# Input projection of a hybrid decoder layer in five column groups instead of six, one of them loaded in two parts

## The chip, the cores and the metric

The kernel runs on one core of a Trainium2 chip. One program does both layers. The metric is the device time of one execution in microseconds (us). One core has five engines that run their own instruction streams in order: PE (TensorE, matrix products; PEld are its weight loads), DVE (VectorE), ACT (ScalarE), POOL (GpSimd) and SP (SyncE), which here only issues DMA transfers. They wait for each other by semaphores.

## The reference

Two layers on x of 256 tokens by 1024, all in float32. The change touches only the input projection, the product of `h` with `w_in` (1024 by 3476 columns per layer), whose columns are split among the three head groups:

```
for l in range(DEPTH):
    h = rmsnorm(x, norm_mix[l])
    proj = jnp.einsum('bsd,de->bse', h, w_in[l]).astype(jnp.float32)
    (m_q, m_k, m_v, m_o, m_i, m_f, b_q, b_k, b_v,
     n_q, n_kc, n_vc, n_ks, n_vs, n_kw, n_vw, n_g) = jnp.split(proj, SPLIT_POINTS, axis=-1)
    ...
    gif = jnp.concatenate([m_i, m_f], axis=-1) + b_if[l]
    y_m = mlstm(..., gif[..., :M_HEADS], gif[..., M_HEADS:], m_norm[l])
    y_b = moba(b_q, b_k, b_v, ...)
    y_n = nsa(n_q, n_kc, n_vc, n_ks, n_vs, n_kw, n_vw, n_g, ...)
    mix = jnp.concatenate([y_m, y_b, y_n], axis=-1).astype(x.dtype)
    x = x + jnp.einsum('bse,ed->bsd', mix, w_out[l])
    h = rmsnorm(x, norm_ffn[l])
    u = jnp.square(jax.nn.relu(jnp.einsum('bsd,df->bsf', h, w_ff1[l])))
    x = x + jnp.einsum('bsf,fd->bsd', u, w_ff2[l])
```

## The kernel before

**How a weight reaches PE.** Weights come in pieces of at most 128 partitions by 1024 elements. For each piece SP issues a DMA into a buffer `raw` (5 buffers), ACT casts it to a rounded copy `hi` (6 buffers), DVE subtracts to get the rest `lo` (6 buffers), and PE makes three passes over it: hi with the high part of the activations H, lo with it, hi with the low part. A `raw` buffer is free once its `lo` is made; `hi` and `lo` are free once PE has used them. The compression weights (`whole`, 2 buffers, two DMAs each into its left and its right half) go to PE uncast.

**How the input projection is staged.** `ORDER` lists, per layer, groups of columns (o1 to o6, each in four pieces of 256 rows of `w_in`), transposed groups (q0 to q3, 256 columns in two pieces) and compression steps (c0 to c3). A group o1 to o6 makes 48 matmuls into two PSUM banks, one for each half of the tokens: 2 halves x 8 blocks of rows x 3 passes, as wide as the group. The pool `acc` has two banks, so the next group takes a bank as soon as it has been read and freed. o1 holds the NSA queries and two compression inputs (384 columns), o6 the mLSTM output gates (512), o2 the other NSA keys, values and gates (268), o3 the mLSTM gate inputs and the MoBA queries (8 + 256 = 264).

**Who reads the banks.** `cmp_inputs` reads o1 into `KV` and `R` (ACT). `nsa_heads(l, i)` reads o2's bank of half i: two ACT copies (`R`, `VS`) and one DVE operation (`GT`), then normalizes (`th`, `hss`, `hr`, `N`) and has PE transpose `N` and `KV`. `gates(l)` reads o3: one DVE operation (`GI`, which needs the small load `BIF`) and one ACT copy into a fresh `R` buffer (2 buffers in the pool). `gates` begins only when the second part of `small_loads` has been read: C, BIF, `sel` (through `th` into `SEL`), CW and MN.

**What sets the order.** Every step is a generator that yields operations; class `Flow` keeps a clock for each engine from estimated costs and picks the next operation greedily, by rank where several could start. It also writes the order of SP's transfers. All instructions go through one helper, so the profile shows line L137 for all of them and L136 for all DMA issues; tiles tell them apart.

Of the kernel before, what the change touches and what calls it, by code (L numbers as in the profile page):

```python
# [10 lines left out]
AF = mybir.ActivationFunctionType  # L11
ALU = mybir.AluOpType
# [9 lines left out]
C_MQ, C_MK, C_MV, C_MO, C_G, C_BQ, C_BK, C_NQ, C_KS = 0, 512, 1024, 1536, 2048, 2056, 2312, 2824, 3208  # L22
# [4 lines left out]
K_ID, K_TRI, K_NM, K_NMT, K_NMC, K_COS, K_SIN, K_VAL, K_CS, K_END = 0, 128, 256, 384, 512, 544, 576, 608, 612, 868  # L27


ORDER = ("o1", "o6", "o2", "o3", "c0", "c1", "q0", "c2", "c3", "o4", "q1", "q2", "q3", "o5")  # L30

RAW_BUFS, PART_BUFS, AHEAD = 5, 6, 1.3

# [111 lines left out]
class Flow:  # L145
# [25 lines left out]
    def free(self, *tiles):  # L171
        for t in tiles:
            name = t.tensor.name
            self.places[self.owner.pop(name)].append(self.used.get(name, ("", 0.0))[1])
# [108 lines left out]
def body(ctx, tc, x, w_in, b_if, conv_qk, m_norm, moba_g, nsa_qg, nsa_kg, cmp_pe, cmp_w1, cmp_w2,  # L283
# [26 lines left out]
    def keep(tag, *shape, dt=F32, parts=128):  # L310

        if tag not in kept:
            kept[tag] = cp.tile([parts, *shape], dt, tag=tag, name=tag)
        return kept[tag]
# [60 lines left out]
    def rows(w, k0, kk, c0, n):  # L375
        return [(w[k0 * 128:(k0 + kk) * 128, c0:c0 + n].rearrange("(k p) n -> p k n", p=128), None)], kk, n

    GROUPS = {"o1": (C_NQ, 384), "o2": (C_KS, 268), "o3": (C_G, 264), "o4": (C_BK, 512), "o5": (C_MV, 512),
              "o6": (C_MO, 512)}
    WO_ORDER = [6, 7, 4, 5, 0, 1, 2, 3]  # L380
    NCH = DFF // 256

# [9 lines left out]
    pieces, due = [], []  # L392
    t = 0.0
    for l in range(DEPTH):
        for name in ORDER:
            if name[0] == "c":
                s = int(name[1])
                pieces.append(([(cmp_w1[l, a, s * 512:(s + 1) * 512, :].rearrange("(k p) n -> p k n", p=128), a)
                                for a in range(2)], 8, 128))
                due.append(t)  # L400
                t += 0.45
            elif name[0] == "q":
                pieces += [rows(w_in[l], 4 * s, 4, int(name[1]) * 256, 256) for s in range(2)]
                due += [t, t + 12 * 288 / 2400]
                t += 48 * 288 / 2400
            else:
                n = GROUPS[name][1]
                pieces += [rows(w_in[l], 2 * s, 2, *GROUPS[name]) for s in range(4)]
                due += [t + 6 * s * (n + 32) / 2400 for s in range(4)]
                t += 48 * (n + 32) / 2400  # L410
        pieces += [rows(w_out[l], k, 1, 0, D) for k in WO_ORDER]
        due += [t + 6 * k * 544 / 2400 for k in range(4)] + [t + (48 + 3 * k) * 544 / 2400 for k in range(4)]
        t += 96 * 544 / 2400
        for kind, c, a in FF_ORDER:
            if kind == "up":
                pieces.append(rows(w_ff1[l], 4 * a, 4, c * 256, 256))
                due.append(t)
                t += (8 * 544 + 8 * 288) / 2400
            else:
                if a == 0:  # L420
                    pieces += [rows(w_ff2[l], 2 * c + f, 1, 0, D) for f in range(2)]
                    due += [t, t + 3 * 544 / 2400]
                t += 12 * 544 / 2400

    whole = {j for j, p in enumerate(pieces) if len(p[0]) == 2}
    raws, parts = {}, {}
    coming = [0, 0]
    taken = [0]
# [1 line left out]
    def loads(unsplit):  # L430

        for j, (srcs, kk, n) in enumerate(pieces):
            if (j in whole) != unsplit:
                continue
            if j < 4:
                yield f"before {j}"
            elif unsplit:
                yield f"raw {j - 1}"
            raw = yield new("whole" if j in whole else "raw", 1024)
            raws[j] = raw  # L440
            for src, a in srcs:
                dst = raw[:, :kk * n] if a is None else raw[:, a * 512:(a + 1) * 512]
                yield sy.dma_start(dst.rearrange("p (k n) -> p k n", n=n), src)
            done.add(f"raw {j}")

    def chunks(j):
# [74 lines left out]
    class Layer:  # L521
        def __init__(self):
            self.o, self.held, self.W, self.Y = {}, {}, {}, {}
            self.rs = [keep(f"rs{i}", 1) for i in range(2)]
            self.r2 = [keep(f"r2{i}", 1) for i in range(2)]
            for name, shape, dt in (("H", (8, 2, S), F32R), ("Mh", (8, S), F32R),
                                    ("Ml", (8, S), F32R), ("QK", (10, S), F32), ("RB", (S,), F32),
                                    ("VS", (2, 2, 64), F32), ("VB", (2, 256), F32), ("VM", (2, 4, 130), F32),
                                    ("VC", (4, 64), F32), ("KCT", (2, 16), F32), ("em", (2, 4), F32),
                                    ("cg", (2, 64), F32), ("mr", (384,), F32R)):  # L530
                setattr(self, name, keep(name, *shape, dt=dt))
            self.GT = [keep(f"GT{i}", 12) for i in range(2)]

            self.Hh, self.Hl = (self.H[:, :, a, :] for a in range(2))
            self.Fh, self.Fl = self.Hh, self.Hl

    Ls = [Layer() for _ in range(DEPTH)]

# [360 lines left out]
    def cmp_inputs(l):  # L899
        L = Ls[l]  # L900
        L.R = []
        KV = []
        for i in range(2):
            yield f"o1{l}{i}"
            yield f"rs{l}{i}"
            o = L.o["o1"][i]
            KV.append((yield new("KV", 2, 2, 64)))
            yield act(KV[i], o[:, 256:384].rearrange("p (a d) -> p a d", a=2)[:, :, None, :].to_broadcast([128, 2, 2, 64]),
                      AF.Copy, scale=L.rs[i])
            L.R.append((yield new("R", 8, 64)))  # L910
            yield act(L.R[i][:, 0:4].rearrange("p a d -> p (a d)"), o[:, 0:256], AF.Copy, scale=L.rs[i])
            free(o)
            done.add(f"R{l}{i}")
        yield f"s0{l}"

        Xt = yield new("MQ", 2048)
        yield gp.memset(Xt[:, :1024], 0.0)
        X = Xt[:, :1024].rearrange("p (i a c) -> p i a c", i=16, a=2)
        for a in range(2):
            kt = yield wk(S)  # L920
            for i in range(2):
                yield tr(kt[:, tokens(i)], KV[i][:, a].rearrange("p b d -> p (b d)"), ident)
            for j in range(2):
                src = kt[64 * j:64 * j + 64, :]
                src = bass.AP(tensor=src.tensor, offset=src.offset + j, ap=[src.ap[0], [2, 16], [16, NCMP]])
                yield tt(X[64 * j:64 * j + 64, :, a, :NCMP], src,
                         PEs[64 * j:64 * j + 64, l, a, :][:, :, None].to_broadcast([64, 16, NCMP]), op=ALU.add)
            free(kt)
        free(*KV)
        L.Xt, L.X = Xt, X  # L930
        done.add(f"X{l}")


    def nsa_heads(l, i):
        L = Ls[l]
        yield f"R{l}{i}"
        yield f"o2{l}{i}"
        yield f"s0{l}"
        o, R, GT = L.o["o2"][i], L.R[i], L.GT[i]
        kv = o[:, 0:256].rearrange("p (a b d) -> p a b d", a=2, b=2)  # L940
        yield act(R[:, 4:6], kv[:, :, 0, :], AF.Copy, scale=L.rs[i])
        yield act(L.VS[:, i], kv[:, :, 1, :], AF.Copy, scale=L.rs[i])

        yield ts(GT, o[:, 256:268], L.rs[i], 0.5, op0=ALU.mult, op1=ALU.mult)
        free(o)
        N = yield new("N", 10, 64)
        yield from normed(N, R[:, 0:6], 6, i, ((0, 4, 2, 1), (4, 2, 4, 2)))
        free(R)
        yield copy(N[:, 6:10, 16:64], N[:, 0:4, 16:64])
        yield from rope(N[:, 4:6], N[:, 4:6], 2, i)  # L950

        K = yield new("KV", 2, 2, 64)
        yield copy(K, N[:, 4:6, None, :].to_broadcast([128, 2, 2, 64]))
        yield from rope(N[:, 6:10], N[:, 0:4], 4, i)
        yield from blocks(L, [N[:, 0:2], N[:, 2:4], K[:, 0], K[:, 1], N[:, 6:8], N[:, 8:10]], 4, i)
        free(N, K)
        yield act(GT, GT, AF.Tanh)
        yield ts(GT, GT, 0.5, 0.5, op0=ALU.mult, op1=ALU.add)
        done.add(f"qkn{l}{i}")
# [43 lines left out]
    def gates(l):  # L1003
# [3 lines left out]
        yield f"s1{l}"  # L1007
        L.R2 = []
        for i in range(2):
            yield f"o3{l}{i}"  # L1010
            yield f"rs{l}{i}"
            o = L.o["o3"][i]
            yield stt(GI[:, i], o[:, 0:8], L.rs[i], BIFs[:, l], op0=ALU.mult, op1=ALU.add)
            L.R2.append((yield new("R", 8, 64)))
            yield act(L.R2[i][:, 0:4].rearrange("p a d -> p (a d)"), o[:, 8:264], AF.Copy, scale=L.rs[i])
            free(o)
            done.add(f"bq{l}{i}")
        fg = GI[:, :, 4:8]
        lf, fa, cg, em, BC = keep("lf", 2, 4), keep("fa", 2, 4), L.cg, L.em, keep("BC", 2, 4)
# [364 lines left out]
```

## Time and profile before

| | |
|---|---|
| median of 3 runs | 640.31 us (639.86 to 641.04) |
| the profiled execution's own time | 639.9 us |
| its span | 638.1 us |
| PE busy | 631.1 us, 99% of the span |
| DVE busy | 443.7 us, 70% |
| ACT busy | 367.0 us, 58% |
| granted TensorE clock, whole span | 1.00 |

The span is the part of the execution that the trace covers; 1.8 us of the profiled execution lie around it. Busy shares are of the span.

### The profile page before, as it was taken

The numbers are of one execution on the slowest core, as the hardware profiler recorded it, in microseconds if no ns is written. First come the engines' busy times: TensorE is split into PE (matmuls) and PEld (weight loads), VectorE is DVE, ScalarE is ACT, GpSimd is POOL, SyncE is SP. The second block draws the span as 40 slices with busy tenths as digits, with TensorE's granted clock in tenths as the row PEclk, the third lists the DMA queues.
The fourth block names the chain that finished last, engine by engine and source line by source line (L and its number), as shares of the span: only waits on it lengthen the run. The fifth ranks groups of instructions, "written<-read, shape, count | busy, mean of one in ns | idle before, by whom it ended". The sixth has DMA issues, their size and how long they took to land.

```text
span 638.1 us, 10222 instructions
## 1 busy us (share of the span) xinstructions
PE 631.1 (99%) x3799; PEld 543.9 (85%) x3799; DVE 443.7 (70%) x823; ACT 367.0 (58%) x718; POOL 29.8 (5%) x50
## 2 busy tenths in 40 slices
PE   8999999999999999999999999999999999999997
PEld 8888898888888888888899979988888888888885
DVE  6679898779575665656593979987776565665661
ACT  7679785556463545445474985945645553545440
POOL 1110200100000000000010111001000000000000
PEclk9999999999999999999999999999999999999999
DMA  8886514448556564656446926145466556564611
GB/s 313 235 287 217 164 67 133 131 133 264 193 185 210 165 213 156 225 166 187 142 140 208 318 68 181 52 133 159 155 214 209 187 185 210 167 215 156 223 33 67
DMA packets 79378, 112.78 MB, mean 177 GB/s; under 512 B 4928, under 2 KB 61792, under 8 KB 79328
## 3 DMA queue, kind: packets, MB, share of 16 engines
q1 hardware_dynamic: 79152, 112.05, 55.4%
q8 instruction: 30, 0.49, 0.3%
q14 instruction: 20, 0.16, 0.1%
q10 hardware_dynamic: 176, 0.07, 0.0%
HBM read 111.06 MB, written 1.05 MB: 176 GB/s over the span
## 4 chain that ended last, share of the span: by engine, by line
PE 95%; DMA 2%; DVE 1%; ACT 1%; issue 0%; POOL 0%; ACTq 0%; DVEq 0%; POOLq 0%
PE wk L137 57%; PE acc L137 38%; DMA raw<-in_w_in 1%; DVE lo L137 1%; DMA ident<-in_cst 1%; ACT hi L137 0%; DVE N L137 0%; POOL rs L137 0%; DVE dg L137 0%; DVE x L137 0%; DVE hss L137 0%; DVE t L137 0%; DVE KC L137 0%; ACT th L137 0%; ACTq L136 0%
## 5 line engine op out<-in xcount | busy, mean ns | idle before, releaser
L137 DVE TENSOR_TENSOR lo<-raw,hi 128x1024 fp32r<-128x1024 f32 (+4 forms) x209 | 240.2, 1166 | 124.1 <-ACT hi L137 122.3
L137 ACT CAST hi<-raw 128x1024 fp32r<-128x1024 f32 (+3 forms) x207 | 205.8, 1015 | 133.3 <-PE wk L137 112.1
L137 PE MATMUL wk<-H,hi 128*128 128x512 f32 x512 | 128.0, 391 | 0.0
L137 PEld LDWEIGHTS wk<-H,hi 128*128 128x128 f32 x512 | 93.7, 188 | 17.9
L137 PE MATMUL acc<-hi,H 128*128 128x512 f32 (+3 forms) x368 | 100.0, 352 | 0.0
L137 PE MATMUL acc<-hi,P 128*128 128x512 f32 x240 | 79.2, 391 | 0.0
L137 PE MATMUL wk<-hi,P 128*128 128x512 f32 x240 | 78.8, 389 | 0.0
L137 PEld LDWEIGHTS wk<-H,lo 128*128 128x128 f32 x512 | 69.9, 190 | 5.0
L137 PE MATMUL wk<-H,lo 128*128 128x256 f32 x512 | 71.4, 282 | 0.0
L137 PEld LDWEIGHTS acc<-hi,H 128*128 128x128 f32 x368 | 63.9, 188 | 6.7 <-issue 0.4
L137 PE MATMUL acc<-lo,H 128*128 128x512 f32 (+3 forms) x184 | 65.2, 354 | 0.0
L137 PEld LDWEIGHTS wk<-hi,P 128*128 128x128 f32 x240 | 45.0, 188 | 9.4
L137 PEld LDWEIGHTS acc<-hi,P 128*128 128x128 f32 x240 | 45.2, 188 | 8.9
L137 PE MATMUL acc<-H,hi 128*128 128x256 f32 x256 | 51.3, 292 | 0.0
L137 PE MATMUL acc<-lo,P 128*128 128x512 f32 x120 | 47.0, 392 | 0.0
L137 PE MATMUL wk<-lo,P 128*128 128x512 f32 x120 | 46.7, 389 | 0.0
L137 ACT COPY th<-wk 128x256 f32<-128x256 f32 x64 | 23.8, 373 | 35.7 <-PE wk L137 35.7
L137 PEld LDWEIGHTS acc<-H,hi 128*128 128x128 f32 x256 | 40.4, 191 | 0.9 <-issue 0.5
L137 PEld LDWEIGHTS acc<-lo,H 128*128 128x128 f32 x184 | 34.6, 188 | 3.6 <-issue 0.7
L137 PE MATMUL acc<-H,lo 128*128 128x256 f32 x128 | 37.4, 292 | 0.1
L137 ACT ACTIVATE H<-wk,V 128x128 fp32r<-128x128 f32 x64 | 18.1, 375 | 21.0 <-PE wk L137 21.0
L137 DVE TENSOR_TENSOR cx<-wk,th 128x256 f32<-128x256 f32 x64 | 26.9, 421 | 2.2 <-ACT th L137 2.2
(199 smaller groups left out, 790.7 us busy)
## 6 DMA issues: line engine op xcount, KB each, us to landing
raw<-in_w_ff SPq DMA_DIRECT2D x128, 512.0 KB, 4.4
raw<-in_w_in SPq DMA_DIRECT2D x40, 512.0 KB, 5.0
raw<-in_w_out SPq DMA_DIRECT2D x16, 512.0 KB, 3.7
whole<-in_cmp_w SPq DMA_DIRECT2D x16, 256.0 KB, 4.9
raw<-in_w_in SPq DMA_DIRECT2D x8, 384.0 KB, 4.0
raw<-in_w_in SPq DMA_DIRECT2D x8, 268.0 KB, 3.5
raw<-in_w_in SPq DMA_DIRECT2D x8, 264.0 KB, 3.3
out<-x SPq DMA_DIRECT2D x4, 256.0 KB, 2.0
```

Source lines behind the costliest of these rows:

```text
L137: o = Op(self.name, lambda: f(out, *args, **kw), outs, ins, self.cost(op, outs, ins))
```

## The change

o3 goes away. o1 takes 64 columns of o2 (the key `ks`) and is 448 wide. What is left of o2 (204 columns) and the 264 of o3 become one group o2 of 468 columns. They are not adjacent in `w_in`, so each of its four pieces is loaded by two DMAs: for each of its two row blocks k, columns 0 to 203 of the piece come from the one and columns 204 to 467 from the other. In the buffer the two parts thus alternate: 204, 264, 204, 264.

`nsa_heads` and `gates` both read o2's bank, and `Layer.read` frees it at the second of the two readers. `cmp_inputs` makes one more copy, of 64 columns, into `R`.

```diff
-ORDER = ("o1", "o6", "o2", "o3", "c0", "c1", "q0", "c2", "c3", "o4", "q1", "q2", "q3", "o5")
+ORDER = ("o1", "o6", "o2", "c0", "c1", "q0", "c2", "c3", "o4", "q1", "q2", "q3", "o5")
...
-    GROUPS = {"o1": (C_NQ, 384), "o2": (C_KS, 268), "o3": (C_G, 264), "o4": (C_BK, 512), "o5": (C_MV, 512),
-              "o6": (C_MO, 512)}
+
+    GROUPS = {"o1": (C_NQ, 448), "o2": (C_KS + 64, 468), "o4": (C_BK, 512), "o5": (C_MV, 512), "o6": (C_MO, 512)}
...
-                pieces += [rows(w_in[l], 2 * s, 2, *GROUPS[name]) for s in range(4)]
+                if name == "o2":
+                    pieces += [([(w_in[l, 256 * s:256 * s + 256, c0:c0 + m].rearrange("(k p) n -> p k n", p=128),
+                                      slice(at, at + m)) for c0, m, at in ((C_KS + 64, 204, 0), (C_G, 264, 204))], 2, n)
+                                   for s in range(4)]
+                else:
+                    pieces += [rows(w_in[l], 2 * s, 2, *GROUPS[name]) for s in range(4)]
...
-                dst = raw[:, :kk * n] if a is None else raw[:, a * 512:(a + 1) * 512]
-                yield sy.dma_start(dst.rearrange("p (k n) -> p k n", n=n), src)
+                dst = raw[:, a * 512:(a + 1) * 512] if j in whole else raw[:, :kk * n]
+                dst = dst.rearrange("p (k n) -> p k n", n=n)
+                yield sy.dma_start(dst[:, :, a] if isinstance(a, slice) else dst, src)
...
+            self.left = [2, 2]
...
+        def read(self, i):
+
+            self.left[i] -= 1
+            if not self.left[i]:
+                free(self.o["o2"][i])
...
+            yield act(L.R[i][:, 4], o[:, 384:448], AF.Copy, scale=L.rs[i])
...
-        yield act(R[:, 4:6], kv[:, :, 0, :], AF.Copy, scale=L.rs[i])
-        yield act(L.VS[:, i], kv[:, :, 1, :], AF.Copy, scale=L.rs[i])
-
-        yield ts(GT, o[:, 256:268], L.rs[i], 0.5, op0=ALU.mult, op1=ALU.mult)
-        free(o)
+        yield act(R[:, 5], o[:, 64:128], AF.Copy, scale=L.rs[i])
+        yield act(L.VS[:, i], o[:, 0:256].rearrange("p (a b) -> p a b", a=2)[:, :, 0:64], AF.Copy, scale=L.rs[i])
+
+        yield ts(GT, o[:, 192:204], L.rs[i], 0.5, op0=ALU.mult, op1=ALU.mult)
+        L.read(i)
...
-            yield f"o3{l}{i}"
+            yield f"o2{l}{i}"
             yield f"rs{l}{i}"
-            o = L.o["o3"][i]
-            yield stt(GI[:, i], o[:, 0:8], L.rs[i], BIFs[:, l], op0=ALU.mult, op1=ALU.add)
+            o = L.o["o2"][i]
+            yield stt(GI[:, i], o[:, 204:212], L.rs[i], BIFs[:, l], op0=ALU.mult, op1=ALU.add)
             L.R2.append((yield new("R", 8, 64)))
-            yield act(L.R2[i][:, 0:4].rearrange("p a d -> p (a d)"), o[:, 8:264], AF.Copy, scale=L.rs[i])
-            free(o)
+            yield act(L.R2[i][:, 0:4].rearrange("p a d -> p (a d)"), o[:, 212:468], AF.Copy, scale=L.rs[i])
+            L.read(i)
```

The planner's order moves in three places. The first is SP's list of transfers in layer 0, from o2's first piece on. Names in brackets are the semaphores that an instruction waits for; DMAHW0 to DMAHW7 are raised by landed transfers, the transfers taking them in turn, and the last number is no time. Before, eight transfers load o2 and o3 (the eighth, alike, stands four rows further):

```order
L136 DMA raw_311<-in_w_in 128x2x268 [waits DMAHW6_49,DVE_49]
L136 DMA raw_336<-in_w_in 128x2x268 [waits DMAHW7_49,DVE_49]
L136 DMA raw_355<-in_w_in 128x2x268 [waits DMAHW0_49,DVE_49]
L136 DMA dg_378<-in_cmp_pe 64x128 [waits DMAHW1_49,PE_49]
L136 DMA raw_367<-in_w_in 128x2x268 [waits DMAHW2_49,DVE_49]
L136 DMA raw_387<-in_w_in 128x2x264 [waits DMAHW3_49,DVE_49]
L136 DMA raw_402<-in_w_in 128x2x264 [waits DMAHW6_49,DMAHW4_49,DVE_49]
L136 DMA raw_408<-in_w_in 128x2x264 [waits DMAHW7_49,DMAHW5_49,DVE_49]
```

Of the change, the same place, where each `raw` is filled by two transfers:

```order
L136 DMA raw_306<-in_w_in 128x2x204 [waits DMAHW6_49,DVE_49]
L136 DMA raw_306<-in_w_in 128x2x264 [waits DMAHW7_49,DMAHW6_49]
L136 DMA raw_333<-in_w_in 128x2x204 [waits DMAHW0_49,DVE_49]
L136 DMA raw_333<-in_w_in 128x2x264 [waits DMAHW1_49,DMAHW0_49]
L136 DMA raw_353<-in_w_in 128x2x204 [waits DMAHW2_49,DVE_49]
L136 DMA dg_368<-in_cmp_pe 64x128 [waits DMAHW3_49,PE_49]
L136 DMA raw_353<-in_w_in 128x2x264 [waits DMAHW4_49,DMAHW2_49]
L136 DMA raw_380<-in_w_in 128x2x204 [waits DMAHW5_49,DVE_49]
L136 DMA raw_380<-in_w_in 128x2x264 [waits DMAHW5_49]
```

A transfer's own semaphore is the first one that it waits for in the first column (the one that it reuses): the first 204 raises DMAHW6, the second DMAHW0, the third DMAHW2 and the fourth DMAHW5. Each 264 therefore waits until the 204 of its own buffer has landed; before, no transfer of this stretch waits for one issued just ahead of it. Behind these rows now come the four `whole`, q0's two pieces and o4's first, and only then C, BIF and `sel`, which before stood ahead of o3's last piece. Layer 1 has the same four pairs.

The second place is ACT, layer 0, around the copies out of o2's and o3's banks (rs0 and rs1 are the scales of the two halves of the tokens). Before, `R_635` reads o3's first bank (acc_571) with three of the casts of q0 and o4 ahead of it:

```order
L137 ACTIVATE VS_74<-acc_525,rs1_94 128x128
L137 CAST hi_559<-raw_467 128x1024 [waits DMAHW0_49]
L137 ACTIVATE th_590<-R_384 128x384 [waits Activation_49]
L137 CAST hi_585<-raw_501 128x1024 [waits DMAHW1_49]
L137 COPY N_540<-N_540 128x4x48 [waits DVE_49]
L137 CAST hi_627<-raw_509 128x1024 [waits DMAHW2_49,PE_49]
L137 COPY KV_638<-N_540 128x256 [waits DVE_49]
L137 ACTIVATE R_635<-acc_571,rs0_93 128x256
```

Of the change, `R_613` reads o2's first bank (acc_487); hi_538, hi_554, hi_567 and hi_580 are the casts of o4's four pieces, and q0's two stand ahead of these rows:

```order
L137 CAST SEL_77<-th_448 128x512 [waits DMAHW0_49]
L137 ACTIVATE R_340<-acc_487,rs0_93 128x64 [waits PE_49]
L137 ACTIVATE VS_74<-acc_487,rs0_93 128x128 [waits DVE_49]
L137 ACTIVATE th_542<-R_340 128x384 [waits Activation_49]
L137 CAST hi_538<-raw_426 128x1024 [waits DMAHW5_49,PE_49]
L137 CAST hi_554<-raw_465 128x1024 [waits DMAHW1_49,PE_49]
L137 CAST hi_567<-raw_477 128x1024 [waits DMAHW2_49,PE_49]
L137 CAST hi_580<-raw_499 128x1024 [waits DMAHW3_49,PE_49]
L137 ACTIVATE R_370<-acc_528,rs1_94 128x64
L137 ACTIVATE VS_74<-acc_528,rs1_94 128x128
L137 ACTIVATE R_613<-acc_487,rs0_93 128x256 [waits DVE_49,Activation_49]
```

All four casts of o4 now stand ahead of the copy, and `VS` waits for DVE, which is `GI` and with it BIF. Layer 1 has the same rows but for `SEL`.

The third place is PE, layer 0, at the end of o2 and the start of q0, of the change. acc_615, q0's, is the place that o2's first bank (acc_487) leaves, so that its first matmul waits for `R_613`:

```order
L137 MATMUL acc_528<-hi_463,H_70 128x468
L137 MATMUL wk_579<-whole_393,MQ_433 32x128 [waits DMAHW7_49,Pool_49]
L137 MATMUL wk_579<-whole_393,MQ_433 32x128 [waits DMAHW0_49]
L137 MATMUL wk_579<-whole_393,MQ_433 32x128 x6
L137 MATMUL wk_579<-whole_403,MQ_433 32x128 [waits DMAHW1_49]
L137 MATMUL wk_579<-whole_403,MQ_433 32x128 [waits DMAHW2_49]
L137 MATMUL wk_579<-whole_403,MQ_433 32x128 x6
L137 MATMUL acc_615<-H_70,hi_475 128x256 [waits PE_49,Activation_49]
```

Before, the rows between `whole` and q0 held two transposes of `N` and two of `KV`; these four now come after 24 of q0's 48 matmuls.

## Rows read from the trace of the kernel before

**Rows 1.** Page, part 1: busy time, share of the span, instructions.

```profile
span 638.1 us, 10222 instructions
...
PE 631.1 (99%) x3799; PEld 543.9 (85%) x3799; DVE 443.7 (70%) x823; ACT 367.0 (58%) x718; POOL 29.8 (5%) x50
```

**Rows 2.** Chain that ended last, 0 to 60 us: start, us, what.

```profile
30.16 7.76 DMA raw<-in_w_in
```

**Rows 3.** Timeline of PE, layer 0: start, us, instruction.

```profile
13.02 0.33 PE L137 MATMUL acc<-lo,H 128*128 128x384 f32 x1
...
14.58 0.36 PE L137 MATMUL acc<-lo,H 128*128 128x384 f32 x1
...
26.66 0.62 PE L137 MATMUL acc<-hi,H 128*128 128x512 f32 x2
...
28.02 0.62 PE L137 MATMUL acc<-hi,H 128*128 128x512 f32 x2
...
29.05 0.28 PE L137 MATMUL acc<-lo,H 128*128 128x268 f32 x1
...
40.67 1.08 PE L137 MATMUL wk<-whole,MQ 128*32 128x128 f32 x32
...
42.48 0.51 PE L137 MATMUL acc<-H,hi 128*128 128x256 f32 x2
...
45.44 0.83 PE L137 MATMUL wk<-QK 64*128 64x128 f32 x10
```

**Rows 4.** Timeline of ACT, layer 0: start, us, instruction, idle before.

```profile
27.48 0.62 ACT L137 CAST SEL<-th 128x512 fp32r<-128x512 f32 x1 [0.40 <-DMA th<-in_sel]
...
32.04 0.37 ACT L137 ACTIVATE R<-acc,rs 128x128 f32<-128x128 f32 x1 [1.64 <-PE acc L137]
...
33.65 0.52 ACT L137 ACTIVATE th<-R 128x384 f32<-128x384 f32 x1
...
41.96 0.47 ACT L137 ACTIVATE R<-acc,rs 128x256 f32<-128x256 f32 x1
42.33 1.99 ACT L137 CAST hi<-raw 128x1024 fp32r<-128x1024 f32 x2
```

**Rows 5.** Tile raw, 26.4 to 26.8 us: o3's last piece.

```profile
L136 SPq DMA_DIRECT2D raw<-in_w_in x1: 379/379/379, 26.5 to 26.5; - x1
...
DMA to landing us min/median/max: 3.0/3.0/3.0
```

**Rows 6.** Timeline of SP, layer 0: start, us, transfers issued.

```profile
15.35 3.06 SPq L136 DMA_DIRECT2D raw<-in_w_in  x3
...
26.89 1.03 SPq L136 DMA_DIRECT2D whole<-in_cmp_w  x2
```

**Rows 7.** Tile raw, 15.2 to 15.7 us: o2's first piece.

```profile
L136 SPq DMA_DIRECT2D raw<-in_w_in x1: 379/379/379, 15.4 to 15.4; - x1
...
DMA to landing us min/median/max: 5.0/5.0/5.0
```

**Rows 8.** Groups by form, 5 to 60 us: busy us, mean ns, idle before.

```profile
L137 ACT CAST hi<-raw 128x1024 fp32r<-128x1024 f32 x12 | 12.5, 1061 | 2.4 <-DMA raw<-in_w_in 2.4
...
L137 DVE TENSOR_TENSOR lo<-raw,hi 128x1024 fp32r<-128x1024 f32 x11 | 13.2, 1216 | 0.6 <-ACT hi L137 0.6
```

**Rows 9.** Windows: length, busy PE, PEld, DVE, ACT, POOL, PEclk, DMA, GB/s.

```profile
32.00:40.00 8.00, 8.00 (x68) 8.00 (x68) 3.38 (x9) 4.88 (x10) 1.34 (x1) 1.00 1.03 337
```

**Rows 10.** Layer 1, timelines of SP and PE.

```profile
321.98 18.98 SPq L136 DMA_DIRECT2D raw<-in_w_in  x9
...
343.12 0.28 PE L137 MATMUL acc<-lo,H 128*128 128x268 f32 x1
```

**Rows 11.** What SP waited for, 320 to 341 us: total, times, longest.

```profile
SPq L136 <- DVE lo L137: 23.8, 8, 9.6
```

**Rows 12.** Window at the end, behind the last matmul; columns as in rows 9.

```profile
633.50:638.00 4.50, 0.00 (x0) 0.00 (x0) 0.75 (x1) 0.00 (x0) 0.00 (x0) 1.00 0.31 118
```

More of the change, by code (lines that the diff above doesn't have):

```diff
@@ L423, in body @@
                 t += 12 * 544 / 2400
-    whole = {j for j, p in enumerate(pieces) if len(p[0]) == 2}
+    whole = {j for j, p in enumerate(pieces) if p[1] == 8}
     raws, parts = {}, {}
@@ L939, in nsa_heads @@
         o, R, GT = L.o["o2"][i], L.R[i], L.GT[i]
-        kv = o[:, 0:256].rearrange("p (a b d) -> p a b d", a=2, b=2)
-        yield act(R[:, 4:6], kv[:, :, 0, :], AF.Copy, scale=L.rs[i])
-        yield act(L.VS[:, i], kv[:, :, 1, :], AF.Copy, scale=L.rs[i])
-        yield ts(GT, o[:, 256:268], L.rs[i], 0.5, op0=ALU.mult, op1=ALU.mult)
-        free(o)
+        yield act(R[:, 5], o[:, 64:128], AF.Copy, scale=L.rs[i])
+        yield act(L.VS[:, i], o[:, 0:256].rearrange("p (a b) -> p a b", a=2)[:, :, 0:64], AF.Copy, scale=L.rs[i])
+        yield ts(GT, o[:, 192:204], L.rs[i], 0.5, op0=ALU.mult, op1=ALU.mult)
+        L.read(i)
         N = yield new("N", 10, 64)
```

## The prediction

> **What bounds the kernel now.** I read the page first: PE is busy for 631.1 of the 638.1 us of the span, DVE and ACT for 70% and 58% [rows 1]. The kernel is as long as PE's list of matmuls, so the change can gain only by shortening that list, and it loses whatever makes PE stand idle. Then I read the chain of waits for the places where PE is nearly late. It leaves PE once behind the start: at 30.16 us a transfer of q0's weights, 7.76 us long, is on it [rows 2]. Layer 0's input projection is thus the one stretch where PE lives from hand to mouth on DMA; from 32 to 40 us the DMA engines are fully used, at 337 GB/s [rows 9]. In layer 1 the same nine loads are spread over 18.98 us and all issued before the work that uses the last of them [rows 10], and SP waits there on DVE giving buffers back, 23.8 us in eight waits: it is ahead, not late [rows 11].
>
> The profiled execution took 639.9 us, 1.8 more than its span; the median is 0.4 above that. I sum against 639.9 and add the 0.4 at the end. A difference under 0.2%, 1.3 us, is about what a measurement of this kernel cannot tell from none.
>
> **The change, part by part.**
>
> *Matmuls.* Three groups of 48 become two. From the timeline, three triples of 384 columns start 1.56 us apart, 0.173 a matmul; two triples of 512 take 1.36, 0.227 each; the 96 of o2 and o3 take 40.67 − 29.05 = 11.62, 0.121 each [rows 3]. On a straight line from 384 to 512, 448 columns cost 0.200 and 468 cost 0.208. Per layer 48 x 0.173 + 11.62 = 19.94 becomes 48 x 0.408 = 19.60: a gain of 0.34, so 0.7 for both layers. Bounds: the steeper line from 266 to 384 (0.00044 a column) gives 0.201 and 0.210, a gain of 0.2; the rate of 512 per column gives 0.198 and 0.207, a gain of 0.5. The extra copy of 64 columns on ACT runs in o6's 12 us and costs nothing.
>
> *Two transfers to a piece, layer 0.* The two parts of a piece alternate in the buffer, and in the order each 264 waits for the landing of its own 204. SP issues in order, so it stands still for that landing, four times per layer, with all later transfers behind it. The trace of before has no such wait, so I bound it by landings: the least crowded comparable load took 3.0 us [rows 5]. With 0.45 for the two issues (two of `whole` take 1.03, [rows 6]) a piece takes 3.45 us of SP. Bounds: 2.3 (3.0 scaled by 204/264) to 3.5 for the landing, so 2.75 to 3.95.
>
> The Trainium skill, "DMA: Bandwidth & Descriptors", section "Anatomy of one DMA — SWDGE (gpsimd) path", gives a transfer a fixed part of about 2.0 us whatever its size, plus bytes over 436 GB/s; by that estimate a 204 KB load takes about 2.5 us, a piece 2.95, and the result below would be about 645.0. The fixed part is what speaks against cutting one load into two that wait for each other.
>
> The first 204 goes out at about 15.95 (15.35 [rows 6], and 0.6 for o1's and o6's buffers coming free later) and lands some 4.75 later at 20.7 (5.0 for the 268 in that place, behind o6's loads [rows 7]). Three periods later, at 31.05, the last 264 goes out; it lands at 34.05. Before, o3's last piece went out at 26.5 and all else of o2 and o3 earlier [rows 5]. Cast and remainder of 128 x 936 take 0.97 and 1.11 (1.06 and 1.22 at 1024, [rows 8], by size) and 0.1 of handing over: piece 3 is ready at 36.2.
>
> PE wants it when? o1 is 48 x 0.027 = 1.3 longer; I let 0.2 of that be absorbed by waits at the start, so o2 starts at 29.05 + 1.1 = 30.15, and wants piece 3 after 18 matmuls, at 33.9. PE stalls 2.3 us, and with 30 matmuls to go o2 ends at T = 42.45. At the low bound the piece is ready by 33 and the stall is nothing (T = 40.15); at the high bound it is some 4.6.
>
> *What is queued behind it.* Behind the last 264 SP has `whole`, q0, o4's first piece, then C, BIF and `sel`: with the 264 itself some 3.2 MB, which at 337 GB/s [rows 9] take 9.5 us. With data flowing about 2 us after 31.05, `sel` lands at about 42.4 (41 to 44.5). o4's other three pieces follow at 1.5 us each, the last near 47.
>
> *The bank with two readers.* q0's first matmul takes the place of o2's first bank and so waits for `gates`' copy `R_613`. ACT reaches that copy only after `SEL` (42.4 to 42.95), the two copies out of the bank (0.5; the first of 128 columns takes 0.37, the second waits for `GI`, and so for BIF), `th` (0.45), the four casts of o4 at 0.95 each with the last not before its landing near 47, two more copies (0.5) and its own 0.47 [rows 4]. That ends at about 49.1. So q0 starts at 49.1; `whole` fills only 1.0 after T, and PE is idle for about 5.6 us.
>
> Before, the same first matmul started at 42.48 [rows 3], right at the end of the same copy (41.96 + 0.47 [rows 4]): it was nearly late already, and the copy has moved. Late are q0 by 6.6 and everything behind it. Two things are taken off or added: the four transposes that stood before q0 are still to come (0.4), and the small stalls that before has behind 42.48 vanish: 15 matmuls at 0.121 and two transposes of 0.1 make 2.0 of the 2.96 us up to 45.44 [rows 3], so 0.9. Layer 0: 6.6 + 0.4 − 0.9 = +6.1 (its gain in matmuls lies in T), by the bounds +4 to +8.5.
>
> *Layer 1.* The four landing waits, some 14 us with their issues, fall into SP's idle 23.8 [rows 11], and o2's end is not delayed. The bank remains: the fourth cast of o4 needs a `hi` buffer that o2's last matmul frees, at T. From there cast 0.95, copies 0.2 and 0.27, `R` 0.47 and handing over 0.15 make 2.05, against 1.0 of `whole`: a wait of 1.0, less the 0.34 gained: +0.7 (0 to +1.2).
>
> **Sum**: 639.9 + 6.1 + 0.7 = 646.7, and with the 0.4 of the median about **647**.
>
> **The rivals.**
>
> *A. The landing waits are hidden in layer 0 too, and the copy is in time.* For it: SP has been far ahead of PE here, with o3's last piece issued at 26.5 [rows 5], some 10 us before PE came to it. It decides where a piece takes SP under 2.6 us (then the last 264 lands before 31.6, in time for PE) and o4's last piece has landed before T. Then both layers gain 0.34 and lose nothing, or little: 639.6 to 639.2 + 0.4, faster by at most 0.7, or by 1.1 at the upper bound of the matmuls with before's stalls gone too: 638.5. Against it: the smallest landing that I found in this stretch is 3.0.
>
> *B. Only the bank's wait stays.* If SP is not held as the order says (the wait on the 204 has passed by the time SP comes to it), each layer waits 1.0 for the copy and gains 0.34; layer 0 also drops its 0.9 of stalls: 639.9 + 1.3 − 0.9 + 0.4 = 640.7, within 0.2%. Against it: SP goes from one half to the next with nothing between them but once.
>
> *C. As forecast*, 644.5 to 649.5 by the landing waits.
>
> *D. As forecast, and TensorE's clock falls in the gap before q0.* Nothing in this trace falls: behind the last matmul PE is idle for 4.5 us and the granted clock stays 1.00 [rows 12]. The gap forecast is 5.6 us, longer than that row can speak for. At the lower of the two levels (1.2 for 2.4 GHz) q0's matmuls cost up to twice 0.121 until the clock is back; if 14 to 28 of q0's 48 are hit, that is 1.7 to 3.4 us more: 648.5 to 650.5. The Trainium skill, "TensorE: Matmul & The Clock Gate", section "What's actually happening", says that an idle engine is throttled and only activity releases it; by that, D is the likelier the longer the gap.
>
> **How the numbers follow.** C 0.62, D 0.24, A 0.06, B 0.08. C and D are slower by over 0.2% but for a tail of C near the low bounds, which I count in B. So slower 0.86, same 0.08, faster 0.06. The likeliest is C at 647.0. The range takes C from its lower bound and D nearly to its end, 644 to 650.5; A, B and the tails outside are under 0.2.
>
> **What the profile of the changed kernel would show.** SP waiting on the landing of `raw` at the 264s, some 3 us each in layer 0; a stall of about 2 us inside o2 of layer 0, released by the `lo` of a 936-wide piece; a gap of about 5 us before q0's first matmul, released by ACT's `R` of 256 columns, with four casts of 1024 just ahead of it; a gap of about 1 us there in layer 1 and none in o2; matmuls of 448 and 468 columns 0.200 and 0.208 apart; a granted clock of 1.00, or under it for D. The forecast is wrong if the 264s go out within half a microsecond of their 204s, if landings there take under 2.3 us, or if the copy `R` finds ACT free at T.

## The result, and the profile of the changed kernel

The changed kernel is slower: 649.81 us (median of 4 runs, 646.65 to 651.55) against 640.29, a ratio of 1.0144 with a 95% interval of 1.0124 to 1.0165. Measured once more beside the last experiment it took 648.2 us (5 runs), a ratio of 1.0128 (1.0106 to 1.0151). So 7.8 to 9.5 us are lost, where 6.7 were forecast, and single executions of the change lie 5 us apart.

The profiled execution of the change is the longest of the four (651.55 us). Its page, part 1:

```profile
span 649.8 us, 10012 instructions
...
PE 635.0 (98%) x3700; PEld 543.4 (84%) x3700; DVE 443.0 (68%) x815; ACT 368.3 (57%) x714; POOL 30.4 (5%) x50
```

PE is busy for 3.9 us more than in [rows 1], although it has 99 instructions less, and idle for 7.8 us more. The timeline of PE in layer 0 (in brackets the idle time before, and what ended it) shows where:

```profile
14.55 0.36 PE L137 MATMUL acc<-lo,H 128*128 128x448 f32 x1
...
17.59 0.36 PE L137 MATMUL acc<-lo,H 128*128 128x448 f32 x1
...
29.14 0.27 PE L137 MATMUL wk<-ident,dg 64*128 64x64 f32 x1 [3.68 <-DMA dg<-in_cmp_pe]
...
37.75 0.38 PE L137 MATMUL acc<-lo,H 128*128 128x468 f32 x1
...
42.22 0.38 PE L137 MATMUL acc<-lo,H 128*128 128x468 f32 x1
...
48.18 1.08 PE L137 MATMUL wk<-whole,MQ 128*32 128x128 f32 x32
53.16 0.50 PE L137 MATMUL acc<-H,hi 128*128 128x256 f32 x2 [3.89 <-ACT R L137]
...
59.92 1.16 PE L137 MATMUL wk<-QK 64*128 64x128 f32 x16
```

Two gaps, 3.68 and 3.89 us. The second is the one forecast, before q0, ended by ACT's `R`. The first is not: it lies inside o6, where PE transposes `cmp_pe`, a small load that SP issues between o2's pieces. There is no stall inside o2 beyond 0.3 us between its two halves. q0 starts at 53.16, where it started at 42.48 [rows 3].

SP's timeline, and what SP waited for from 15 to 50 us (total, times, longest):

```profile
17.84 8.57 SPq L136 DMA_DIRECT2D raw<-in_w_in  x5
26.51 0.51 SPq L136 DMA_DIRECT2D dg<-in_cmp_pe  x1
28.94 3.87 SPq L136 DMA_DIRECT2D raw<-in_w_in  x3
```

```profile
SPq L136 <- DMA raw<-in_w_in: 10.9, 5, 3.8
```

Five of o2's eight transfers take 8.57 us of SP; before, three loads of its pieces took 3.06 [rows 6]. SP stands 10.9 us waiting for `raw` to land, and `cmp_pe`, which has to do with none of it, goes out behind five of them. The chain of waits (start, us, what) confirms that this is the path:

```profile
22.55 2.98 DMA raw<-in_w_in
...
26.00 2.92 DMA raw<-in_w_in
...
29.41 3.02 DMA raw<-in_w_in
...
35.33 5.76 DMA raw<-in_w_in
```

Three landings of a 204, one after the other, then q0's first piece; before, one transfer of 7.76 stood there [rows 2].

ACT's timeline behind that, to be read as [rows 4]:

```profile
46.59 0.62 ACT L137 CAST SEL<-th 128x512 fp32r<-128x512 f32 x1 [2.70 <-DMA th<-in_sel]
...
48.40 3.87 ACT L137 CAST hi<-raw 128x1024 fp32r<-128x1024 f32 x4
...
52.63 0.48 ACT L137 ACTIVATE R<-acc,rs 128x256 f32<-128x256 f32 x1
```

`sel` lands at 46.6, four casts stand ahead of the copy, the copy ends at 53.11 and q0 starts at 53.16. From `sel` on ACT is idle for only 0.3 us until the copy has ended, so the landing of `sel` sets q0's start here.

Windows of PE (length, busy, granted clock, DMA, GB/s) behind the two gaps:

```profile
29.14:33.60 4.46, 4.46 (x16) 0.62 0.41 112
53.16:57.30 4.14, 4.14 (x22) 0.59 1.03 309
```

The clock fell to its lower level behind both. At full clock the same matmuls would take some 1.7 us less in each window (4.46 x 0.38 and 4.14 x 0.41), an estimate that covers 3.4 of the 3.9 us by which PE is busier. Layer 1, PE's timeline:

```profile
366.08 1.08 PE L137 MATMUL wk<-whole,MQ 128*32 128x128 f32 x32
368.12 0.50 PE L137 MATMUL acc<-H,hi 128*128 128x256 f32 x2 [0.96 <-ACT R L137]
```

One gap of 0.96 us there, as forecast, and nothing else.

### The profile page after: what moved, and what is told of

Its sections match the earlier page's. It is cut to its first block, busy times and chain, and to the rows that moved or that the text cites. A ratio compares the mean times of both kernels' runs of the same rounds, so it can differ in the third digit from the quotient of the medians.

```text
span 649.8 us, 10012 instructions
## 1 busy us (share of the span) xinstructions
PE 635.0 (98%) x3700; PEld 543.4 (84%) x3700; DVE 443.0 (68%) x815; ACT 368.3 (57%) x714; POOL 30.4 (5%) x50
## 4 chain that ended last, share of the span: by engine, by line
PE 91%; DMA 3%; issue 2%; ACT 1%; SPq 1%; DVE 1%; POOL 0%; ACTq 0%; POOLq 0%
PE wk L137 54%; PE acc L137 37%; DMA raw<-in_w_in 3%; SPq L136 1%; ACT hi L137 1%; DVE lo L137 0%; POOL rs L137 0%; ACT R L137 0%; ACT H L137 0%; DVE H L137 0%; DVE dg L137 0%; DVE x L137 0%; ACT g L137 0%; ACT VS L137 0%; ACT RB L137 0%
## 5 line engine op out<-in xcount | busy, mean ns | idle before, releaser
L137 DVE TENSOR_TENSOR lo<-raw,hi 128x1024 fp32r<-128x1024 f32 (+3 forms) x201 | 239.4, 1207 | 131.8 <-ACT hi L137 131.0
L137 ACT CAST hi<-raw 128x1024 fp32r<-128x1024 f32 (+2 forms) x199 | 203.9, 1049 | 144.3 <-PE wk L137 111.8
L137 PE MATMUL acc<-hi,H 128*128 128x512 f32 (+2 forms) x304 | 99.9, 399 | 0.1
L137 PEld LDWEIGHTS acc<-hi,H 128*128 128x128 f32 x304 | 57.3, 192 | 9.2 <-issue 0.7
L137 PE MATMUL acc<-lo,H 128*128 128x512 f32 (+2 forms) x152 | 60.1, 395 | 0.1
L137 PEld LDWEIGHTS acc<-lo,H 128*128 128x128 f32 x152 | 29.1, 192 | 4.1 <-DVE lo L137 0.3
```

Source lines behind the costliest of these rows:

```text
L137: o = Op(self.name, lambda: f(out, *args, **kw), outs, ins, self.cost(op, outs, ins))
```

## The experiments

Ratios are to the kernel before, run on the same chip beside each (medians 641.17, 640.54 and 640.42 us).

**The landing wait alone.** The same program, with o2's rows 472 columns apart in the buffers:

```diff
-                dst = raw[:, a * 512:(a + 1) * 512] if j in whole else raw[:, :kk * n]
-                dst = dst.rearrange("p (k n) -> p k n", n=n)
+                if isinstance(a, slice):
+                    dst = raw[:, :2 * 472].rearrange("p (k n) -> p k n", n=472)
+                else:
+                    dst = raw[:, a * 512:(a + 1) * 512] if j in whole else raw[:, :kk * n]
+                    dst = dst.rearrange("p (k n) -> p k n", n=n)
```

and the same rows in `hi` and `lo`. SP's list, at the place shown ahead of the prediction, then begins:

```
L136 DMA raw<-in_w_in 128x2x204 [waits DMAHW6_49,DVE_49]
L136 DMA raw<-in_w_in 128x2x264 [waits DMAHW7_49]
```

> The changed kernel with one thing else: a row of o2's buffers is 472 columns apart in raw, hi and lo, not 468, so four columns between the rows stay unused. The same 16 transfers go out in the same order, but none of the 264s waits for its 204 any more; all other instructions and their order are those of the changed kernel. Theory (SP's landing waits cause nearly all of the loss in layer 0): the stall of 3.7 us for cmp_pe in o6, the gap before q0 but for about 1 us, and both falls of the clock go away; layer 1 keeps its 1.0 us; 641 to 643.5 us. Rival (the cost is in the number and the size of the transfers, or in the bank with two readers): at least 646.

640.48 us, 0.9992 (0.9980 to 1.0004): the kernel before's own time, 0.5 under the theory's range. The one wait is worth some 9 us (1.36 and 1.52% by the change's two ratios). PE's timeline and SP's wait, 15 to 50 us:

```profile
25.01 0.27 PE L137 MATMUL wk<-ident,dg 64*128 64x64 f32 x1 [0.82 <-DMA dg<-in_cmp_pe]
...
44.17 0.50 PE L137 MATMUL acc<-H,hi 128*128 128x256 f32 x2 [0.96 <-ACT R L137]
```

```profile
SPq L136 <- DMA raw<-in_w_in: 0.8, 3, 0.3
```

10.9 us of waiting became 0.8, both gaps shrank to under a microsecond, and q0's is now what it is in layer 1. Why 468 makes the framework order the two parts and 472 does not, I did not find out; the parts share no element in either.

**The same in layer 0 alone**, 468 kept in layer 1 (the edit above, with 472 for the first half of the pieces).

> The changed kernel with rows 472 columns apart in layer 0 alone; in layer 1 each 264 still waits for its 204. Theory (layer 1's landing waits fall into time in which SP had nothing to do): the same as with 472 in both layers, 640 to 641. Rival (layer 1 pays for its waits too): 642 or more, with a stall in layer 1's o2 or a longer one before its q0.

640.42 us, 0.9996 (0.9987 to 1.0005). Its SP still waits in layer 1, from 322 to 345 us:

```profile
SPq L136 <- DVE lo L137: 10.6, 2, 9.4
SPq L136 <- DMA raw<-in_w_in: 10.3, 4, 2.7
```

The waits for landings have taken the place of waits for buffers (23.8 us of these before, [rows 11]) and cost nothing, as forecast.

**`cmp_pe` early.**

```diff
         yield "H017"
+        per = MN[:, :128]
+        yield sy.dma_start(per[:64], cmp_pe.rearrange("l a (i j) d -> (l a i) (j d)", j=2))
         yield from small_loads(0, 0)
```

> The changed kernel, with cmp_pe's transfer sent ahead of o2's pieces (into MN's buffer, which is free then), so that PE's transpose of it is not late. The landing waits stay. Theory (the whole stream of transfers is late by the waits, and cmp_pe only meets it first): the stall of 3.7 us in o6 goes, but the time comes back as a stall in o2 and a longer gap before q0; 646.5 to 649.5. Rival (each stall has its own cost, and they add): about 644.5, the 3.7 us and the 1.7 us of the clock behind it taken off.

650.93 us, 1.0149 (1.0128 to 1.0169): 1.4 above the theory's range and no faster than the change. PE's timeline:

```profile
34.94 0.48 PE L137 MATMUL acc<-hi,H 128*128 128x468 f32 x1 [1.39 <-ACT hi L137]
36.10 0.76 PE L137 MATMUL acc<-lo,H 128*128 128x468 f32 x1 [0.69 <-DVE lo L137]
...
52.29 0.79 PE L137 MATMUL acc<-H,hi 128*128 128x256 f32 x2 [5.93 <-ACT R L137]
```

The 3.7 us are gone from o6 and stand in o2 and before q0, where they had been forecast, 1.4 (and 0.7 for a `lo`) and 5.9 us. So the first gap of the change is not added to the second: PE loses there what it would wait for later. q0 starts at 52.29. This program's planner also put C, BIF and `sel` ahead of o2's last 264; `sel` landed at 33.4, but q0 gained nothing by it, since the four casts then waited for o4's own landings. The late thing is the whole stream of transfers, not one small load.

**Another bank.**

```diff
-                po.append((yield new("wk" if l == 0 and name == ORDER[1] and i == 0 else "acc", 512)))
+                po.append((yield new("wk" if i == 0 and (l == 0 and name == ORDER[1] or name == "o2") else "acc", 512)))
```

> The changed kernel, with o2's first bank taken from the pool wk, so that q0's first matmul takes a bank that nobody has to read first. Theory (ACT's copy out of the shared bank ends the gap before q0 in both layers, but in layer 0 the normalized keys that PE transposes next are as late as that copy): layer 1 gains its 1.0 us, layer 0 some 2 to 3, with a new wait for N; 645.5 to 647.5. Rival (the bank alone makes the gap): 643, both gaps and the second fall of the clock gone. Rival (the bank is not what q0 waits for): no change, 649 to 651.

645.28 us, 1.0071 (1.0050 to 1.0092), 0.2 under the theory's range. Its PE waits for nothing from 45 to 70 us, and q0 starts right behind `whole`:

```profile
47.58 1.08 PE L137 MATMUL wk<-whole,MQ 128*32 128x128 f32 x32
48.59 0.51 PE L137 MATMUL acc<-H,hi 128*128 128x256 f32 x2
```

The new wait for `N` that I expected did not come, because the planner moved here too: the transposes of `N` stand behind 34 of q0's matmuls, not 24. The gap before `cmp_pe` (3.81 us) and the slow clock behind it are still there. The bank, with the order that comes with it, is thus worth some 4 us beside the landing waits (0.57% and 0.73% by the change's two ratios). That includes the 1.0 us of layer 1. It is the bank through which the late stream reaches q0.

**Both edits.**

> Both edits: rows of 472 columns (no landing wait) and o2's first bank from the pool wk. Theory: what remains of the change is the start of layer 0, which is some 2 us later in its profile, against no stall in o2, o3 and q0: 640 to 642. Rival (fewer and wider matmuls give 0.3 us per layer as forecast, and the late start was chance): 638.5 to 639.5, faster than before.

638.3 us, 0.9955 (0.9939 to 0.9970): faster than both kernels, under the theory's range and under the rival's. Against the landing wait's edit alone the bank, with the same move of the transposes, gives 2.2 us; each layer's wait of 1.0 is gone. Span 635.7 us; PE's timeline:

```profile
40.98 1.08 PE L137 MATMUL wk<-whole,MQ 128*32 128x128 f32 x32
41.99 0.51 PE L137 MATMUL acc<-H,hi 128*128 128x256 f32 x2
```

q0 starts 0.5 us earlier than before. The rival's reason is not borne out, since the matmuls are no cheaper (below).

**Rows 512 apart, with that bank.**

> Rows 512 columns apart in o2's buffers, so that each starts at a multiple of 2 KB, and o2's first bank from wk; otherwise as the kernel with 472 and that bank. Theory (the 0.213 of a 468-column matmul is its width): the same time as with 472, 637.5 to 639. Rival (the row's offset in the buffer is what makes 468 dearer than the straight line from 384 to 512 says): 0.208 a matmul and 0.4 us less.

638.23 us, 0.9965 (0.9952 to 0.9978): as with 472. A matmul of 468 takes 0.2115 us instead of 0.212, so the row's offset is not what makes it dear.

**The widths alone**, in the kernel before, with the copies out of the banks to match (one more for `ks`, and `VS` in two parts):

```diff
-    GROUPS = {"o1": (C_NQ, 384), "o2": (C_KS, 268), "o3": (C_G, 264), "o4": (C_BK, 512), "o5": (C_MV, 512),
+    GROUPS = {"o1": (C_NQ, 448), "o2": (C_KS + 64, 204), "o3": (C_G, 264), "o4": (C_BK, 512), "o5": (C_MV, 512),
```

> The kernel before with the first part of the change alone: the 64 columns of ks go from o2 (268, then 204) to o1 (384, then 448). Still six groups, one transfer to a piece, o3 by itself, every bank with one reader. Theory (what a matmul costs at these widths gives next to nothing): 48 x 0.203 for o1 and, between 0.098 and 0.121 for a matmul of 204 columns, a change of +1.4 less 0 to 1.1 us per layer; 640 to 642.5. Rival (wider groups are cheaper per column, and the merged kernel's gain without its waits comes from the widths): at or under 639.

641.65 us, 1.0024 (1.0011 to 1.0036): 1.5 us slower by the ratio. Its o2 in layer 1, PE's timeline:

```profile
345.20 0.28 PE L137 MATMUL acc<-lo,H 128*128 128x204 f32 x1
...
350.23 0.27 PE L137 MATMUL acc<-lo,H 128*128 128x204 f32 x1
```

15 triples in 5.03 us are 0.112 a matmul. 64 columns less than 268 save 0.009, 64 more than 384 cost 0.030: 48 x 0.021 = 1.0 us per layer lost by the matmuls' prices. Joining 204 and 264 into one of 468 gives that back (0.112 + 0.122 against 0.213) and no more.

**The clock.** In the changed kernel, small matmuls for PE while it waits:

```diff
+            fill = yield wk()
+            for _ in range(64):
+                o = mm(fill[:, 0:128], idb, idb, start=True, stop=True)
+                o.cost = 1e-9
+                yield o
+            free(fill)
```

ahead of q0's first matmul in layer 0, and 60 of the same ahead of `cmp_pe`'s transpose; they cost the planner nothing, so that its order stays.

> The changed kernel with 60 small bf16 matmuls into an unused bank ahead of PE's wait for cmp_pe and 64 ahead of q0's first matmul, which keep PE busy while it waits; nothing else moves. Theory (the clock falls because PE stands idle in the two gaps, and the slow stretches behind them cost 1.7 us each): granted clock 1.00 throughout, both gaps filled, and 3 us under the changed kernel, 645.5 to 647. Rival (the clock's fall has another cause, or costs nothing since PE waits again later): 648.5 to 651.

648.73 us, 1.0132 (1.0112 to 1.0152): not the 3 us, and by its interval not told apart from the change. In its profiled execution the clock is 1.00 in every stretch. Columns of this window: length, busy PE, PEld, DVE, ACT, POOL, clock, DMA, GB/s:

```profile
24.00:33.00 9.00, 9.00 (x43) 7.03 (x42) 5.42 (x10) 2.73 (x4) 0.00 (x0) 1.00 0.56 155
```

PE without work is thus what makes the clock fall, as far as one execution shows it; in two of the other four the mean clock of the span was 0.996, lower than in any execution of the kernel before beside them (0.998 to 1.000), so it may have fallen there. Keeping it up did not bring the time. PE's timeline, and ACT's copy:

```profile
34.52 0.38 PE L137 MATMUL acc<-lo,H 128*128 128x468 f32 x1
...
41.02 0.48 PE L137 MATMUL acc<-hi,H 128*128 128x468 f32 x1 [1.43 <-ACT g L137]
...
50.89 0.48 PE L137 MATMUL acc<-H,hi 128*128 128x256 f32 x2
```

```profile
50.32 0.47 ACT L137 ACTIVATE R<-acc,rs 128x256 f32<-128x256 f32 x1
```

o2 starts 3.2 us earlier than in the change's profile (37.75), but PE then waits 1.4 us in it for a bank of o6, and q0 still starts only when the copy has ended, at 50.79. What PE loses in o6, by the gap or by the clock, is hidden behind that copy. I then filled the second gap alone, beside the unedited change.

> The changed kernel once more, unedited, beside the next. Theory (its profiled execution started late: o1's last matmul at 19.85, where five other kernels with the same start have it at 18.1 to 18.6): about 1.4 us less before o2, and 648 to 650 us. Rival (that start is part of the change): o1's last matmul at 19.8 again and 650 to 652.

> The changed kernel with only the second set of small matmuls, 64 ahead of q0's first matmul in layer 0. Theory (q0's start is set by the late transfers and by ACT, so that the first fall of the clock, in o6, is hidden, and only the fall behind the gap before q0 costs time): 1.5 to 2 us under the changed kernel measured beside it. Rival (both falls cost alike, and filling one leaves half): 1.7 us with both filled worth 3.4; the kernel with both sets would then have to lie 1.7 us lower than this one. Rival (the fall costs nothing): no difference.

The change took 648.2 us, the filled one 649.36 (ratios 1.0128 and 1.0135, with overlapping intervals): no gain. The repeated change's PE timeline, and windows behind its two gaps:

```profile
28.16 0.27 PE L137 MATMUL wk<-ident,dg 64*128 64x64 f32 x1 [4.17 <-DMA dg<-in_cmp_pe]
...
50.44 0.51 PE L137 MATMUL acc<-H,hi 128*128 128x256 f32 x2 [2.26 <-ACT R L137]
...
55.71 1.16 PE L137 MATMUL wk<-QK 64*128 64x128 f32 x16
```

```profile
28.50:32.00 3.50, 3.50 (x11) 0.51 0.48 137
50.44:54.00 3.56, 3.56 (x30) 1.00 1.03 303
```

Here the clock fell behind the first gap alone. The wait before q0 is shorter than in the first profile (2.26 for 3.89) because `sel` landed earlier, at 43.87, and with it the copy. Behind the second gap the clock fell in one of the two profiles of the change, and there it cost 1.5 us: from q0's first matmul to the products of `QK` it took 53.16 to 59.92, 6.76 us, against 5.27 here.

The kernel with the second gap filled does not show what is saved when this fall is avoided, because the small matmuls themselves held q0. Its copy, on ACT, and q0's first matmul:

```profile
51.08 0.48 ACT L137 ACTIVATE R<-acc,rs 128x256 f32<-128x256 f32 x1
```

```profile
52.20 0.48 PE L137 MATMUL acc<-H,hi 128*128 128x256 f32 x2
```

The copy ended at 51.56, and q0 started 0.64 us later, behind the last of the 64.

In the repeated execution o1's last matmul starts at 18.37, not 19.85 as in the first, so the late start was chance; q0 starts at 50.44, within 1.4 us of the forecast 49.1.

## Why the prediction was right, step by step

Direction, path and most of the size were right: 647 with a range of 644 to 650.5, against 649.8 and 648.2.

- *The 264 waits for its own 204, about 3.0 us.* Shown. The eight transfers landed in 2.8 to 4.2 us, median 2.9; the last 264 went out at 32.4 and, in the repeated run, at 31.4, where 31.05 was forecast. A piece took SP 3.45 and 3.41 us (22.55, 26.00 and 29.41 in the chain above), where 3.45 was forecast; the 0.45 in it is one issue, not the two that the prediction names. Undoing this one wait undoes the loss.
- *A stall of 2.3 us inside o2.* Wrong in place. I had read SP's list for what stands behind the last 264 and not for what stands between: `cmp_pe`, which PE transposes in o6, was an instruction moved past in the queue, and I gave it no term. PE lost 3.7 to 4.2 us there, and o2 came late enough to need no stall: it started at 37.75 (36.77 in the repeated run) where 30.15 was forecast, and ended at 48.18 (47.10) where T was 42.45. The sum did not suffer, since q0 waits for the copy and not for T. With `cmp_pe` early, o2 did stall, for 2.1 us in all.
- *`sel` at 42.4, and 6.7 us of ACT behind it.* The ACT part was 6.5 us (46.59 to 53.11). `sel` landed at 46.6 and, in the repeated run, at 43.9. This is the term that was too small, by 1.5 to 4.2 us: 1.4 of the larger figure is the later last 264; for the rest, between the issue of the last 264 and the landing of `sel` the DMA engines moved 305 GB/s for 14.15 us (294 for 12.47 in the repeated run), some 4.3 and 3.7 MB where I had counted 3.2; o4's pieces, issued behind `sel`, flow beside it.
- *q0 waits for the copy.* Shown by the other bank: without it, q0 follows `whole` directly.
- *Layer 1: landings hidden, 1.0 us for the bank.* Both shown, at 0 and 0.96.
- *0.34 us per layer gained in matmuls.* Mis-sized: it is nothing. In the change five triples of 448 take 3.04 us, 0.203 a matmul, and seven of 468 take 4.47, 0.213, so 48 x 0.416 = 19.95 us against 19.94. Both lie above the line from 384 to 512, which gives 0.200 and 0.208.
- *Rival B.* With rows 472 columns apart its condition is met, no landing wait and the bank's wait alone. B's sum was 640.7; that kernel took 640.48.
- *Rival D, the clock.* In the first profile it came true: the clock fell in q0, for 1.5 us, where 1.7 to 3.4 had been put for 14 to 28 slow matmuls, a number that no row of before gives. In the repeated profile it did not. The mean clock of the span divides the nine executions of the change: three at 0.996 or 0.997 took 646.65 to 647.27 us, six at 0.992 to 0.995 took 648.2 to 651.55. That fits D in the longer six, the medians among them, but only two of the nine have a profile, and the filled kernels do not settle it. So how much of the median's distance from 647 is D's stays open.
- *Why single executions differ.* The two profiled ones are 4.3 us apart, and their traces account for 4.2: 1.0 by which the last 264 goes out later, with the late start; 1.7 by which `sel` then takes longer to land; 1.5 of the clock in q0.
- *The sum.* The repeated profile took 647.27, and 646.7 had been summed. That is closer than its parts, and so in part luck: q0 came 1.3 us later than forecast, and from q0's start to the end of the span it took 595.06 us, where 595.62 of before and the summed 0.2 (0.4 − 0.9 + 0.7) make 595.8, so 0.8 less. Which work saves the 0.8 is not shown.

The Trainium skill, "DMA: Bandwidth & Descriptors", section "Anatomy of one DMA — SWDGE (gpsimd) path", has a fit by which a 204 KB load would land in about 2.5 us, an estimate; the fit is for transfers that GpSimd issues. Here SP issues them, and the 204s behind the first took 2.92 to 3.02 (the chain above), so the measured landings decide. That most of a small transfer's time does not shrink with its size agrees with what is seen: the 32 KB of `cmp_pe` landed in 2.6 us, the 204 and 264 KB behind the first in 2.8 to 3.0.

That the merged kernel without its two waits is faster than before by 0.4% is measured; that it comes from the stalls around q0, which before still has, is argued from q0's earlier start and not shown by a run of its own. Its trace does say where the time goes: from the first `whole` to the second it takes 9.3 us in either layer, where before takes 12.3 and 10.8. Part of this is work that the planner moved behind the second `whole`, for of the 2.7 us that it is ahead of before there in layer 0 it has lost 1.1 again by the first `whole` of layer 1.

## What to carry to other kernels

Where one load becomes two into the same buffer, read the order for a wait between the two: on an in-order queue it costs a whole landing each time (some 3 us here), and the bill goes to everything behind it, small loads that another engine needs included. Follow the stream that is late to the last thing it reaches; stalls upstream of that are the same loss seen early, and mending one of them alone brought nothing here (650.93 us with `cmp_pe` early). A bank with two readers comes free at the later reader's place in its own engine's order, so it matters what that engine has been told to do first.

## What the runs showed of the hardware

- One fp32r matmul, start to start: 0.112 us for 204 columns, 0.122 for 264, 0.121 for 268, 0.173 for 384, 0.203 for 448, 0.213 for 468, 0.227 for 512. Wider is not cheaper per column all along: 204 + 264 cost 0.234 apart and 0.213 together, but 268 + 384 cost 0.294 and 204 + 448 cost 0.315.
- The granted clock was at its lower level (0.50 to 0.62 over the stretch) in the 3.5 to 4.6 us looked at behind gaps of 3.7, 3.8, 3.9, 4.2 and 5.9 us in which PE did nothing. It stayed at 1.00 behind gaps of 0.96 and 2.26 us, and through the 4.5 us without a matmul at the end of the kernel before [rows 12]. The longest gap alone does not decide: with `cmp_pe` early it fell (0.52 from 36.1 to 39.6 us) behind waits of 1.39 and 0.69 us with one matmul between them. With small matmuls ahead of both gaps it stayed at 1.00 in the execution that was profiled.
